# Where tiles begin in SBUF: a different start of weights and of moving operands within 512 bytes

## The chip, the core and the metric

The kernel runs on one core of a Trainium2 chip. The metric is the device time of one execution in microseconds (us), lower is better. Engines are named as in the profile: PE (TensorE matmuls), PEld (TensorE weight loads), DVE (VectorE), ACT (ScalarE), POOL (GpSimd), SP (the engine that issues most DMAs).

## What is computed

A decoder trunk of four layers on one sequence of 256 tokens, 1024 wide, in float32. Each layer is

```python
x = x + 0.5 * swiglu(rmsnorm(x), w_gu, w_down)      # ffn1, hidden width 2816
x = x + mixer(rmsnorm(x))                           # gated DeltaNet, stick-breaking, sparse, gated DeltaNet
x = x + 0.5 * swiglu(rmsnorm(x), w_gu, w_down)      # ffn2
```

and a last rmsnorm follows. Nearly all the work is in the products with the weights: in each of the eight feed-forward blocks 1024 x 5632 and 2816 x 1024, in each mixer the input and output projections.

## The kernel before

**Operands.** Everything is kept transposed, features on the 128 partitions and tokens along them, so a product has weights as its stationary operand (loaded by PEld) and activations as its moving operand (read by PE). A float32 operand is split into two float32r parts, hi and lo, and one product becomes three matmuls, hi*hi, lo*hi and hi*lo, added in PSUM (`mm3`, line 49).

**Weights.** `chunk` (line 160) brings 128 x 2048 float32 by one DMA of SP into a tile `r` (3 buffers) and splits it into four pieces of 512 columns: ACT writes `h` (line 170), DVE writes `l` (line 171), ten buffers of each. A weight load reads 128 columns of `h` or `l`, 512 bytes in each partition, at a multiple of 512 bytes from the piece's start. The exceptions are few: loads of 96 columns from the sparse mixer's `dsa_uk` pieces, at 0, 384, 768 and 1152 bytes of a piece; loads of 16 columns (`bah`, `bal`, DeltaNet's gates) and 8 columns (`wih`, `wil`, the sparse mixer's index weights) from small tiles; and the values' products of two mixers, where activations are loaded and weights are the moving operand of 512 columns.

**Moving operands.** `x2` holds the normed input, for each of the 8 k tiles 256 columns hi and 256 columns lo side by side (lines 215 to 223). In the feed-forward blocks `tile_wide` (line 284) multiplies a weight tile's hi part by all 512 columns and its lo part by the hi 256, two matmuls per k tile into a bank of kind G. `tiles2` (line 274) does the mixers' projections with three matmuls of 256 columns. `rows` (line 295) does the second product of a feed-forward block, whose moving operands are `ah` and `al` (256 columns each, into the four banks of kind A), and the output projections, whose moving operands are `oh` and `ol` (into banks of kind G). `lath` and `latl` are the sparse mixer's latents. The smaller products of the mixers use plain float32 or 16-bit tiles.

**Order.** One program order is written out by hand: big products in a row, and between groups of them `pump` (line 130) runs the next stages of side work (gates, norms, attention heads) whose due time, on a clock that `Bank.mm` counts, has come. The engines follow that order and wait for one another by semaphores. The change does not touch it, nor the number of buffers of any tile.

**Places in SBUF.** Tiles are laid one pool behind the other in each partition, in the order in which the pools are made (lines 72 to 77), and within a pool one group of buffers behind the other. The constants begin at byte 16,512 and take 16,096 bytes. So the pool of `r` begins at 32,608, which is 352 modulo 512. Behind it come 3 x 8192 bytes of `r`, 10 x 2048 of `h`, 10 x 2048 of `l`, 16,384 of `x2`, 8 x 8192 of the tiles called `b8` (`oh`, `ol`, `lath`, `latl`, queries, keys and others), and 6 x 2048 of the 512-column working tiles `w5`: all are multiples of 512, so every one of these tiles begins at 352 modulo 512. Then small tiles of 2240 bytes come in between, and `ah` (6 x 1024) and `al` (6 x 1024) lie at 32 modulo 512. `wih` and `bah` begin at 0 modulo 512.

In what follows the distance of a matmul is the start of its moving operand less the start of the weights that are loaded while it runs (those of the matmul after it), modulo 512. It is 0 for all big products on `x2`, `oh`, `ol`, `lath`, `latl`, and 192 for those on `ah` and `al`.

```python
    def mm3(self, out, w, x, stop):
        self.mm(out, w[0], x[0], False)
        self.mm(out, w[1], x[0], False)
        self.mm(out, w[0], x[1], stop)
```

Of the kernel before, what the change touches and what calls it, by code (L numbers as in the profile page):

```python
# [20 lines left out]
P = 128  # L21
T = 256          # tokens
D = 1024
KT = D // P      # k tiles of the model width
F = 2816
NS = F // 256    # steps of a feed-forward block, 256 hidden columns each
# [3 lines left out]
RS = 1024.0      # scale of the residuals kept in float16  # L30

# Everything is kept transposed: [feature on partitions, token].  A float32 matmul operand x is split
# exactly into hi = x rounded to float32r and lo = x - hi; hi*hi + lo*hi + hi*lo in PSUM carries float32.


class Bank:
    """One PSUM bank that several accumulation groups share."""
# [16 lines left out]
    def tr(self, out, x):  # L54
        """Transposes a [128, 128] float32 tile; the only kind of write to its part of the bank."""
        self.nc.tensor.transpose(out, x, self.k.ident)  # L56
        self.k.now += 0.11
# [8 lines left out]
class Trunk:  # L66

    def __init__(self, tc, ctx, a):
        self.tc, self.nc, self.a = tc, tc.nc, a
        nc = self.nc  # L70
        pool = lambda **k: ctx.enter_context(tc.tile_pool(**k))
        self.const = pool(name="const", bufs=1)
        self.raw = pool(name="raw", bufs=3)
        self.hip = pool(name="hi", bufs=10)
        self.lop = pool(name="lo", bufs=10)
        self.big = pool(name="big", bufs=8)
        self.wk = pool(name="wk", bufs=2)
        self.ps = pool(name="ps", bufs=4, space=bass.MemoryType.PSUM)
        self.side, self.now = [], 0.0
        self.act_set("silu_and_others")  # L80
        c = self.const
        self.x = c.tile([P, KT, T], F32, name="x")
        self.gains = c.tile([P, 13, KT], F32, name="gains")
        self.ones = c.tile([P, P], F32, name="ones")
        nc.gpsimd.memset(self.ones, 1.0)
        self.ident = c.tile([P, P], F32, name="ident")
        bf = c.tile([P, 2, P], BF16, name="bf")
        self.identb, self.scap = (bf[:, i] for i in range(2))
        hf = c.tile([P, 3, P], F16, name="hf")
        self.identh, self.identk, self.m1 = (hf[:, i] for i in range(3))  # L90
        self.consts = ((self.ident, a["ident"]), (bf, a["bf"]), (hf, a["hf"]))
        self.pad = c.tile([P, T], F32, name="pad")
        nc.gpsimd.memset(self.pad, 0.0)
        self.pcs = [c.tile([P, 2, 3 + T], F32, name="pc%d" % i) for i in range(2)]
        for pc in self.pcs:
            nc.gpsimd.memset(pc[:, :, :3], 0.0)

    def table(self, name):
        """A mixer's constants, side by side."""
        t = self.wk.tile([P, 1024], F32, name="tab", tag="tab", bufs=1)  # L100
        src = self.a[name]
        self.nc.sync.dma_start(t[:, :src.shape[1]], src)
        return t
# [4 lines left out]
    def w5(self, name, dt=F32):  # L108
        return self.wk.tile([P, 512], dt, name=name, tag="w5", bufs=6)

    def w2(self, name, dt=F32, tag="wa"):
        return self.wk.tile([P, 256], dt, name=name, tag=tag, bufs=6)
# [4 lines left out]
    def bank(self, tag="A"):  # L117
        """A: small products and a feed-forward's sums; G: the big projections."""
        return Bank(self, self.ps.tile([P, 512], F32, name="bank" + tag, tag=tag))

    # ---- interleaving: side work (generators) advances between groups of the big products.  A generator
    # yields how long (us on TensorE's clock, as counted here) its next stage's operands are expected to take,
    # or a condition that its next stage waits for.
# [6 lines left out]
    def pump(self, n=None):  # L130
        """Run up to n ready stages; only the first few (width) generators are under way."""
        for _ in range(n or self.burst):
            g = min(self.side[:self.width], key=self.due, default=None)
            if g is None or self.due(g) > self.now:
                return
            self.step(g)
# [8 lines left out]
    def wait(self, done):  # L145
        """Run side work until done()."""
# [13 lines left out]
    def chunk(self, src, w=2048, pw=512, pool=(), parts=1):  # L160
        """A [128, w] chunk of weights as (hi, lo) pieces of pw columns; the pieces in pool are split by GpSimd."""
# [12 lines left out]
    def first_chunk(self, src, n):  # L174
        """The kernel's start: the first chunk and x arrive in parts and are split as they come."""
# [27 lines left out]
    def rsqrt(self, a, n):  # L203
        """Newton's iteration for a ** -0.5 on a small tile."""
# [20 lines left out]
    def norm_in(self, n):  # L225
        """x times the gain, split; the tokens' factors come later (rstd)."""
# [5 lines left out]
    def spread(self, cols):  # L232
        """[token, 1] columns (SBUF) -> a bank with each as a row on all partitions."""
# [5 lines left out]
    def rstd(self, st):  # L239
        """1 / rms(x) per token, into st: compact [token, 2] and as rows [128, T]."""  # L240
# [28 lines left out]
    # GDN's chunks of the input projection, (kind, head pair): keys 0, values 1, queries 2, gate 3  # L269
    gdn_order = ((0, 0), (0, 1), (0, 2), (3, 0), (0, 3), (3, 1), (2, 0), (1, 0), (1, 1), (1, 2), (1, 3),  # L270
                 (2, 1), (3, 2), (2, 2), (2, 3), (3, 3))
    korder = (0, 2, 4, 6, 1, 3, 5, 7)    # the order in which a block's last products finish x

    def tiles2(self, pieces, xg, order=None):
        """Two M tiles (8 k tiles each) of one chunk into one bank."""
# [8 lines left out]
    def tile_wide(self, pieces, m, order=None):  # L284
        """One M tile into a bank: the columns of hi * hi and those of hi * lo + lo * hi side by side."""
# [9 lines left out]
    def rows(self, acc, pieces, a2, last, done=None):  # L295
        """acc[d, t] += w[f, d] a[f, t] for the chunk's two k tiles."""
# [73 lines left out]
    def gdn(self, i, n):  # L370
# [17 lines left out]
        # b and a: [16, T]  # L388
# [4 lines left out]
        # pairs (head, chunk of tokens) are kept in the order of the projections: head pair, chunk, head of the pair  # L393
# [13 lines left out]
        def gates():  # L407
# [29 lines left out]
            # E[j, i] = exp(G_i - G_j) for i >= j, else 0; eGb: exp(G_i) of the second chunk as rows  # L437
# [13 lines left out]
        def conv2(b, kind, c, dst):  # L451
            """Convolution and silu of two projected heads: dst [128, 2, T]."""
# [3 lines left out]
            # chunks are stored k, v, q; the convolution's channels q, k, v  # L456
# [18 lines left out]
        def keys(c):  # L475
# [23 lines left out]
            # A = I + L (unit lower triangular), transposed, in two float16 parts  # L499
# [8 lines left out]
            # the inverse X of A in float16 by merging blocks; XT its transpose  # L508
# [26 lines left out]
            # float32: with R = I - A X, the inverse is X + X R + X R R (+ X R^3, below float32)  # L535
# [7 lines left out]
            X1 = self.wk.tile([P, 4, P], F16, name="X1", tag="wb", bufs=6)  # L543
# [38 lines left out]
        def delta(c):  # L582
# [36 lines left out]
            # the queries' factor s = dk^-0.5 / |q| goes into the output's norm: s * rsqrt(s^2 ss/128 + eps)  # L619
# [53 lines left out]
    def sb(self, n):  # L673
# [31 lines left out]
        def attend(h, qk):  # L705
            # z^T: [keys, queries]; columns: key tile 0 x all queries, key tile 1 x queries of tile 1
# [38 lines left out]
    def rms_factor(self, sq, n, ones, out):  # L745
        """rsqrt(mean of squares + eps) per token from a squared tile, into out [token, 2]."""
# [11 lines left out]
    def dsa(self, n):  # L758
# [15 lines left out]
        # tiles of the input projection: cq 0..2, index key | rotary key 3, ckv 4..5; 6: the normed index key  # L774
# [25 lines left out]
        def weights():  # L800
            """A query's weights of the index heads, times the factor of its latent, which relu lets through."""
# [6 lines left out]
        def latents(c, b):  # L808
            """Evacuate a chunk of the input projection: factor of the token, squares, gain and split."""
# [21 lines left out]
        def index_keys():  # L831
            """kidx[:, e]: the rotated index key in the rows of a tile's head e, zeros in the other's; rotary keys into K."""
# [49 lines left out]
        def select():  # L882
            """The 64 largest of each row are struck out; what is struck out and causal is selected: neg 0, else -1e30."""
# [33 lines left out]
        def attend(h):  # L917
# [21 lines left out]
            for i in range(3):       # (key 0, query 0), (key 0, query 1), (key 1, query 1)  # L939
# [26 lines left out]
        # the index first, so that the selection runs beside the projections of queries, keys and values  # L966
# [61 lines left out]
    def final(self, out):  # L1028
        """The last norm, beside the last products: to be called with each tile of x as it is done."""
# [53 lines left out]
def cols(w):  # L1083
    """[1024, n * 256] -> [n, 128, 2048]: per chunk two M tiles of 8 k tiles."""
# [4 lines left out]
def rows(w):  # L1089
    """[n * 256, 1024] -> [n, 128, 2048]: per chunk two k tiles."""  # L1090
# [4 lines left out]
def pack_ffn(gu, down):  # L1095
    out = np.empty((gu.shape[0], NS, 3, 128, 2048), gu.dtype)
    for l in range(gu.shape[0]):
        # a chunk: gate tile, up tile
# [6 lines left out]
def feat(g):  # L1105
    """[n * 128] -> [128, n]"""
    return g.reshape(-1, 128).T


def pack(x, ffn1_norm, ffn1_w_gu, ffn1_w_down, mix_norm, ffn2_norm, ffn2_w_gu, ffn2_w_down,  # L1110
# [41 lines left out]
    # constants of the shapes  # L1152
# [10 lines left out]
    for v, s in enumerate((2, 4, 8, 16, 32, 64)):  # L1163
        c = np.arange(64)
        blk = c // s                      # block of 2s of the c-th first-half column
# [41 lines left out]
```

## Time and profile before

| what | value |
|---|---|
| time, median of 3 runs | 2089.65 us (2089.23 to 2093.7) |
| the profiled execution, span from first to last instruction | 2092.3 us |
| PE busy | 2037.1 us, 97% |
| DVE busy | 1646.0 us, 79% |
| ACT busy | 1308.2 us, 63% |
| mean busy share of the 16 DMA engines, by the main queue's packets | 48.4% |
| mean granted TensorE clock | 0.993 |

The profiled execution has no time of its own beside its span; the span lies inside the spread of the timed runs. Matmuls are pipelined: a matmul's row shows a duration of some 280 ns for 256 columns, but the next one starts 113 to 120 ns later. How fast the products go is therefore read from the starts in the timeline or from a run of matmuls in the chain of work, not from the mean duration of one.

### The profile page before, as it was taken

The numbers are of one execution on the slowest core, as the hardware profiler recorded it, in microseconds if no ns is written. First come the engines' busy times: TensorE is split into PE (matmuls) and PEld (weight loads), VectorE is DVE, ScalarE is ACT, GpSimd is POOL, SyncE is SP. The second block draws the span as 40 slices with busy tenths as digits, with TensorE's granted clock in tenths as the row PEclk, the third lists the DMA queues.
The fourth block names the chain that finished last, engine by engine and source line by source line (L and its number), as shares of the span: only waits on it lengthen the run. The fifth ranks groups of instructions, "written<-read, shape, count | busy, mean of one in ns | idle before, by whom it ended". The sixth has DMA issues, their size and how long they took to land.

```text
span 2092.3 us, 38898 instructions
## 1 busy us (share of the span) xinstructions
PE 2037.1 (97%) x14762; PEld 1886.2 (90%) x14762; DVE 1646.0 (79%) x3456; ACT 1308.2 (63%) x2804; POOL 161.9 (8%) x145
## 2 busy tenths in 40 slices
PE   8999899999999999999999998999999998999998
PEld 7999899999999989999989997899989998999997
DVE  7778898877887776777787789877787788988776
ACT  6566776665665566655665664765665667766654
POOL 1001311100100010100010013100010013111000
PEclk9999999999999999999999999999999999999999
DMA  7555333555455554555555542455555553235552
GB/s 256 195 188 182 102 105 123 173 190 187 171 206 188 195 179 140 176 184 197 185 184 199 182 153 76 162 187 196 184 182 199 184 179 106 100 119 182 182 199 84
DMA packets 52603, 353.62 MB, mean 169 GB/s; under 512 B 6976, under 2 KB 7872, under 8 KB 10688
## 3 DMA queue, kind: packets, MB, share of 16 engines
q1 hardware_dynamic: 52128, 350.49, 48.4%
q8 instruction: 116, 1.90, 0.4%
q14 instruction: 71, 0.58, 0.1%
q10 hardware_dynamic: 288, 0.66, 0.1%
HBM read 350.07 MB, written 1.05 MB: 168 GB/s over the span
## 4 chain that ended last, share of the span: by engine, by line
PE 82%; DVE 12%; ACT 4%; issue 1%; POOL 0%; DMA 0%; SPq 0%; ACTq 0%; DVEq 0%; POOLq 0%
PE bankG L43 55%; PE bankA L43 25%; DVE l L171 5%; ACT x L222 1%; DVE kT L466 1%; PE bankA L56 1%; ACT h L170 1%; DVE x L223 1%; DVE rs_t L211 1%; DVE x L302 0%; DVE rs_y L212 0%; DVE rs_t L210 0%; ACT sq L244 0%; DVE vT L466 0%; DVE pc L455 0%
## 5 line engine op out<-in xcount | busy, mean ns | idle before, releaser
L43 PE MATMUL bankG<-x,h 128*128 128x512 f32 (+1 forms) x4192 | 1269.0, 361 | 12.0 <-DVE x L223 12.0
L171 DVE TENSOR_TENSOR l<-r,h 128x512 fp32r<-128x512 f32 x1328 | 936.7, 713 | 374.1 <-ACT h L170 370.9
L170 ACT ACTIVATE h<-r 128x512 fp32r<-128x512 f32 x1328 | 823.0, 627 | 595.5 <-PE bankG L43 337.4
L43 PE MATMUL bankG<-x,l 128*128 128x256 f32 x3504 | 989.2, 282 | 0.0
L43 PEld LDWEIGHTS bankG<-x,h 128*128 128x128 f32 x4192 | 751.3, 189 | 130.1 <-DVE x L223 14.9
L43 PEld LDWEIGHTS bankG<-x,l 128*128 128x128 f32 x3504 | 666.5, 190 | 0.1
L43 PE MATMUL bankA<-ah,l 128*128 128x256 f32 x1408 | 389.2, 276 | 0.0
L43 PE MATMUL bankA<-ah,h 128*128 128x256 f32 x1408 | 389.2, 276 | 0.0
L43 PE MATMUL bankA<-al,h 128*128 128x256 f32 x1408 | 389.1, 276 | 0.0
L43 PEld LDWEIGHTS bankA<-ah,h 128*128 128x128 f32 x1408 | 264.4, 188 | 3.3
L43 PEld LDWEIGHTS bankA<-al,h 128*128 128x128 f32 x1408 | 264.5, 188 | 0.0
L43 PEld LDWEIGHTS bankA<-ah,l 128*128 128x128 f32 x1408 | 264.4, 188 | 0.0
L330 DVE TENSOR_TENSOR e<-e,bankG 128x256 f32<-128x256 f32 x352 | 145.9, 414 | 4.6 <-ACT e L329 4.6
L329 ACT ACTIVATE e<-bankG 128x256 f32<-128x256 f32 x352 | 129.3, 367 | 11.5 <-PE bankG L43 11.5
L245 POOL TENSOR_TENSOR sq<-sq 128x512 f32<-128x512 f32 x12 | 15.5, 1294 | 1473.8 <-ACT sq L244 1473.8
L342 DVE TENSOR_TENSOR e<-e,rb 128x512 f32<-128x512 f32 x176 | 121.0, 691 | 5.3 <-ACT rb L259 0.2
L199 ACT ACTIVATE ah<-e 128x256 fp32r<-128x256 f32 x176 | 72.6, 417 | 21.4 <-DVE e L344 21.3
L343 ACT ACTIVATE e<-e 128x256 f32<-128x256 f32 x176 | 71.3, 405 | 7.2 <-DVE e L342 7.2
L43 PE MATMUL bankG<-oh,h 128*128 128x256 f32 x256 | 74.5, 291 | 0.0
L344 DVE TENSOR_TENSOR e<-e 128x256 f32<-128x256 f32 x176 | 73.8, 419 | 0.7 <-ACT e L343 0.7
L200 DVE TENSOR_TENSOR al<-e,ah 128x256 fp32r<-128x256 f32 x176 | 73.1, 419 | 0.5 <-ACT ah L199 0.5
L43 PE MATMUL bankG<-oh,l 128*128 128x256 f32 x256 | 72.5, 283 | 0.0
(290 smaller groups left out, 1704.7 us busy)
## 6 DMA issues: line engine op xcount, KB each, us to landing
r<-in_ffn SPq DMA_DIRECT2D x262, 1024.0 KB, 4.9
r<-in_gdn_in SPq DMA_DIRECT2D x32, 1024.0 KB, 4.9
r<-in_gdn_out SPq DMA_DIRECT2D x8, 1024.0 KB, 4.9
r<-in_sb_qk SPq DMA_DIRECT2D x8, 1024.0 KB, 4.9
r<-in_sb_v SPq DMA_DIRECT2D x4, 1024.0 KB, 4.9
r<-in_sb_out SPq DMA_DIRECT2D x4, 1024.0 KB, 4.9
r<-in_dsa_out SPq DMA_DIRECT2D x4, 1024.0 KB, 4.9
r<-in_dsa_in SPq DMA_DIRECT2D x3, 1024.0 KB, 4.8
```

Source lines behind the costliest of these rows:

```text
L43: self.nc.tensor.matmul(out, lhsT, rhs, start=self.fresh, stop=stop, skip_group_check=True)
L56: self.nc.tensor.transpose(out, x, self.k.ident)
L170: self.nc.scalar.activation(h[:, :pw], src, AF.Copy)
L171: (self.nc.gpsimd if pool else self.nc.vector).tensor_sub(l[:, :pw], src, h[:, :pw].bitcast(F32))
L199: self.nc.scalar.activation(dh, src, AF.Copy)
L200: self.nc.vector.tensor_sub(dl, src, dh.bitcast(F32))
L211: nc.vector.scalar_tensor_tensor(t, t, -0.5, a, op0=ALU.mult, op1=ALU.mult)
L329: nc.scalar.activation(e[:, m * T:(m + 1) * T], b.t[:, :T], AF.Copy)
L330: nc.vector.tensor_add(e[:, m * T:(m + 1) * T], e[:, m * T:(m + 1) * T], b.t[:, T:])
L342: nc.vector.tensor_mul(e2, e2, st["rb"][:, None, :].to_broadcast([P, 2, T]))
L343: nc.scalar.activation(e[:, :T], e[:, :T], AF.Silu)
L344: nc.vector.tensor_mul(e[:, T:], e[:, T:], e[:, :T])
```

## The change

Two tiles that nothing uses are put in, one of 160 bytes per partition ahead of the pool of `r` and one of 256 bytes behind the pool of `l`, and the 512-column and 256-column working tiles get pools of their own behind the `b8` tiles, with the same six buffers for each tag. `X1`, which shared its buffers with `al`, goes along.

```diff
@@ Trunk.__init__
         self.const = pool(name="const", bufs=1)
+
+        pool(name="gap", bufs=1).tile([P, 40], F32, name="gap")
         self.raw = pool(name="raw", bufs=3)
         self.hip = pool(name="hi", bufs=10)
         self.lop = pool(name="lo", bufs=10)
+        pool(name="gap1", bufs=1).tile([P, 64], F32, name="gap1")
         self.big = pool(name="big", bufs=8)
+        self.w5p = pool(name="w5p", bufs=6)
+        self.w2p = pool(name="w2p", bufs=6)
         self.wk = pool(name="wk", bufs=2)
...
     def w5(self, name, dt=F32):
-        return self.wk.tile([P, 512], dt, name=name, tag="w5", bufs=6)
+        return self.w5p.tile([P, 512], dt, name=name, tag="w5")
 
     def w2(self, name, dt=F32, tag="wa"):
-        return self.wk.tile([P, 256], dt, name=name, tag=tag, bufs=6)
+        return self.w2p.tile([P, 256], dt, name=name, tag=tag)
...
-            X1 = self.wk.tile([P, 4, P], F16, name="X1", tag="wb", bufs=6)
+            X1 = self.w2p.tile([P, 4, P], F16, name="X1", tag="wb")
```

Comments are taken out too, which compiles to nothing. No instruction, no size and no order changes. With 160 more bytes `r` begins at 32,768, a multiple of 512, and so do `h` and `l`; with 256 more `x2`, `oh`, `ol`, `lath`, `latl` and `w5` begin at 256 modulo 512, and `ah` and `al`, which now follow `w5` directly, too. The distance of all big products becomes 256. All other tiles of the last pool move by 416 bytes modulo 512, as `x2` and the `b8` tiles do, so their places relative to those stay.

## Rows read from the trace of the kernel before

**Rows 1.** The page: span, and busy time, share and instructions of PE and DVE.
```profile
span 2092.3 us, 38898 instructions
...
PE 2037.1 (97%) x14762; PEld 1886.2 (90%) x14762; DVE 1646.0 (79%) x3456; ACT 1308.2 (63%) x2804; POOL 161.9 (8%) x145
```

**Rows 2.** The page: the chain that ended last, by engine and by line.
```profile
PE 82%; DVE 12%; ACT 4%; issue 1%; POOL 0%; DMA 0%; SPq 0%; ACTq 0%; DVEq 0%; POOLq 0%
```

**Rows 3.** Chain in order of time, a feed-forward block: start us, us, matmuls in one piece.
```profile
52.53 5.45 PE bankA L43 x48
57.97 11.10 PE bankG L43 x64
```

**Rows 4.** PE's timeline in a DeltaNet projection (start us, us, instruction): distance 0.
```profile
247.82 0.28 PE L43 MATMUL bankG<-x,l 128*128 128x256 f32 x1
...
248.90 0.28 PE L43 MATMUL bankG<-x,l 128*128 128x256 f32 x1
```

**Rows 5.** PE's timeline, index weights: loads of 8 columns, moving operand in x2.
```profile
1244.73 0.28 PE L43 MATMUL bankA<-x,wil 128*8 128x256 f32 x1
...
1245.75 0.28 PE L43 MATMUL bankA<-x,wil 128*8 128x256 f32 x1
...
1246.10 0.28 PE L43 MATMUL bankA<-x,wil 128*8 128x256 f32 x1
```

**Rows 6.** PE's timeline in the values' products of the stick-breaking mixer: 512 columns, distance 0.
```profile
752.21 0.39 PE L43 MATMUL bankG<-l,x 128*128 128x512 f32 x1
...
753.57 0.39 PE L43 MATMUL bankG<-l,x 128*128 128x512 f32 x1
```

**Rows 7.** Groups by line, shapes apart: count, busy us, mean ns | idle before.
```profile
L43 PE MATMUL bankG<-x,h 128*128 128x512 f32 x2816 | 990.2, 394 | 11.7 <-DVE x L223 11.7
L43 PE MATMUL bankG<-x,l 128*128 128x256 f32 x3504 | 989.2, 282 | 0.0
...
L43 PE MATMUL bankA<-ah,h 128*128 128x256 f32 x1408 | 389.2, 276 | 0.0
...
L43 PE MATMUL bankG<-x,h 128*128 128x256 f32 x1376 | 278.9, 292 | 0.2 <-DVE x L223 0.2
...
L43 PE MATMUL bankG<-oh,h 128*128 128x256 f32 x256 | 74.5, 291 | 0.0
...
L43 PE MATMUL bankG<-lath,h 128*128 128x256 f32 x36 | 10.7, 297 | 0.0
```

**Rows 8.** PE's timeline, plain float32 products: distance 0 (kT), then 192 (u).
```profile
243.76 0.83 PE L43 MATMUL bankA<-kT 128*128 128x128 f32 x6
...
354.29 0.94 PE L43 MATMUL bankA<-u,E 128*128 128x128 f32 x7
```

**Rows 9.** Groups by line on DVE: all at 352 (L344), and with al, ah at 32 (L200).
```profile
L344 DVE TENSOR_TENSOR e<-e 128x256 f32<-128x256 f32 x176 | 73.8, 419 | 0.7 <-ACT e L343 0.7
L200 DVE TENSOR_TENSOR al<-e,ah 128x256 fp32r<-128x256 f32 x176 | 73.1, 419 | 0.5 <-ACT ah L199 0.5
```

**Rows 10.** Busy us in a feed-forward stretch: PE, PEld, DVE, ACT, POOL, clock, DMA share.
```profile
390.00:570.00 180.00, 179.35 (x1215) 164.44 (x1214) 138.84 (x265) 110.96 (x227) 2.89 (x3) 1.00 0.56 192
```

**Rows 11.** PE's timeline, dsa_uk: loads of 96 columns at distances 0, 128, 256, 384.
```profile
1287.02 0.28 PE L43 MATMUL bankG<-lath,l 128*96 128x256 f32 x1
...
1288.08 0.27 PE L43 MATMUL bankG<-lath,l 128*96 128x256 f32 x1
1288.19 0.28 PE L43 MATMUL bankG<-latl,h 128*96 128x256 f32 x1
```

**Rows 12.** Busy us, clock and DMA share as in rows 10, of 3.2 us in dsa_uk.
```profile
1283.40:1286.60 3.20, 3.20 (x18) 3.20 (x17) 3.17 (x17) 1.11 (x2) 1.28 (x1) 0.50 0.03 5
```

**Rows 13.** PE's timeline inside the stretch of rows 12.
```profile
1283.61 0.41 PE L43 MATMUL bankG<-latl,h 128*96 128x256 f32 x1
...
1284.03 0.41 PE L43 MATMUL bankG<-lath,l 128*96 128x256 f32 x1
```

## Prediction

> **What bounds the kernel now.** I read the page first: PE is busy 97% of the span, DVE 79% [rows 1]. Busy time of pipelined matmuls proves little, so the chain that ended last comes next: 82% of it is PE [rows 2]. The reader is to see that almost every microsecond is paced by one matmul following another, so the question is what sets the step from start to start. The chain in order of time gives that step inside a feed-forward block [rows 3]. The second products (`ah`, `al`, distance 192) run 48 matmuls in 5.45 us, 113.5 ns each for 256 columns. The first products (`x2`, distance 0) run 64 in 11.10 us; 32 of them have 512 columns and 32 have 256, so one pair takes 346.9 ns. The timeline of a DeltaNet projection, also at distance 0, has nine steps of 256 columns in 1.08 us, 120 ns each [rows 4]. The same size of matmul thus costs 113.5 or 120 ns, and the clock doesn't explain it (granted 1.00 in a feed-forward stretch, 2.4 GHz [rows 10]).
>
> Two things differ between the two paces: the distance, and the PSUM banks (kind A, kind G). The index weights help to tell them apart: moving operand in `x2`, as in the products at 120 ns, but with loads of only 8 columns. Their nine steps from 1244.73 to 1245.75 take 1.02 us, 113 ns each [rows 5]. So the place of `x2` alone does not make a matmul slow. A long weight load from an unlucky place does, or bank G does, since these products go to bank A. I take the first reading: the load of the next weights and the moving read run side by side from one partition's memory, and starts that agree modulo 512 get in each other's way.
>
> **The change part by part.**
>
> *Products at distance 0 that go to 256, with 256 columns.* In [rows 7] the projections have 1376 with `x,h` and 3504 - 2816 = 688 with `x,l`; the output projections have three groups of 256; the latents' loads of 128 columns three groups of 36. That is 2064 + 768 + 108 = 2940. If 256 serves as well as 192 does, each step falls from 120 to 113.5 ns: 2940 x 6.5 ns = 19.1 us.
>
> *The 2816 pairs of 512 and 256 columns.* They take 346.9 ns now [rows 3]. What 512 columns cost without a collision, no row shows. One end: a fixed 113.5 - 106.7 = 6.8 ns above the columns' time for a matmul of any width (106.7 is 256 columns at 2.4 GHz; at 1.2 GHz the same products step by 0.42 us in two, 210 ns each, which is 256 columns and no excess, [rows 12, 13]). Then 512 columns cost 220.1, the pair 333.6, and the gain is 2816 x 13.3 ns = 37.5 us. Other end: the excess grows with the columns, 512 cost 227, the pair 340.5, and the gain is 2816 x 6.4 = 18.0 us. The nearest row is the values' product: 512 columns, six steps in 1.36 us, 226.7 each, and that at distance 0 [rows 6]. It fits the second end, with no collision left in a matmul long enough to cover its load. I take 18.0 us, and nothing for the values' products themselves.
>
> *The second products, from distance 192 to 256.* There are 3 x 1408 = 4224 [rows 7]. They are at the floor already; I take 0. The bounds are no gain below 113.5, and +6.5 ns each if 256 collides as 0 does (rival 2).
>
> *Working tiles, other engines, DMAs.* The plain float32 products don't care: six at distance 0 begin and end within 0.83 us, seven at 192 within 0.94; with 275 ns for the last, both give 111 ns a step [rows 8]. Zero for them. DVE takes 419 ns for 256 columns whether its tiles lie at 352 or at 32 [rows 9]; zero there too. DMAs, their number and order stay, and the DMA engines are busy 56% in a feed-forward stretch [rows 10]. Buffer counts stay, so no wait is added and none removed.
>
> *Does the gain reach the end?* In a feed-forward stretch of 180 us PE is busy 179.35, DVE 138.84, ACT 110.96 [rows 10]. PE's work there would shrink by about 2%, to some 176 us; DVE keeps more than 35 us of slack, which is the cover that the whole gain stands on. What is late next would be DVE's splitting `l`, but only if PE lost over a fifth. In the mixers some waits on side work grow by what the products give back; I take off nothing, as it is a part of at most a few us.
>
> *Sum.* 19.1 + 18.0 = 37.1 us. The traced span of 2092.3 becomes 2055.2. The median of the runs is 2089.65, 2.65 us lower, so against it the forecast is 2052.5.
>
> **A rule against it.** The rows show two paces for one shape, 113.5 and 120 ns [rows 3, 4]. The Trainium skill, "SBUF — State Buffer", section "Who interferes with whom", says that PE has two independent read ports, one for the moving operand and one for weight loads, and that PE never waits on anyone. By that rule places in SBUF cost PE nothing and the sum would be 0; it is rival 3 below. The rows don't refute it, since bank and distance differ together.
>
> **Rivals.**
>
> 1. *The excess is fixed per matmul.* The pairs gain 37.5 us, the sum is 19.1 + 37.5 = 56.6, the time 2033. For it: uniform. Against: 226.7 ns for 512 columns would then hide a second collision [rows 6]. Beyond it lies one more case: starts at multiples of 256 bytes instead of 32 past a multiple of 64 might remove the 6.8 ns itself. In units of 256 columns there are 2 x 2816 + 3504 + 1376 + 4224 + 768 + 108 = 15,612 of them, 106 us at most. The index weights' loads begin at many places and never go below 113 [rows 5], but their moving operand doesn't move. I give it 4%.
>
> 2. *256 is as bad as 0 (slower).* What counts may be the distance modulo 128 or 256, and then 192 was a lucky place. The big products on `x2` keep their pace, and the 4224 second products fall from 113.5 to 120 ns: 27.5 us, from 2089.65 to 2117. It decides from the first feed-forward block on, and all of it is in the runs of 48. For it: the `dsa_uk` products load 96 columns at distances 0, 128, 256 and 384, and the nine steps from 1287.02 to 1288.08 average 118 ns, so the places other than 0 gain little [rows 11]. Also, among the index weights' loads at eight places, the three steps from 1245.75 to 1246.10 take 117 ns where the nine before took 113; there the load begins at 96, which is just the distance 256 [rows 5]. Against: the one step of 110 ns in `dsa_uk` (1288.08 to 1288.19) is also the third and last with a load at 256 under way, as if the products were settling into a good place; the change of distance every three matmuls lets none of the four settle. And 192, which is close to 256, is good in 4224 cases, where 128 and 384 stand on the side of 0. If nearness to 0 is what hurts, 256 is the best place.
>
> 3. *Nothing.* The bank kind, not the place, makes the difference, or the loss at distance 0 has another cause. Then 2090. For it: all fast rows go to banks A. Against: no row shows anything that would make one kind of bank slower than the other.
>
> **How the numbers follow.** The forecast has 0.45, rival 1 with its extreme 0.11 (0.07 and 0.04), rival 2 has 0.32, rival 3 has 0.12. What a measurement of this kernel can tell from no change is about 0.2%, 4 us. So faster is 0.45 + 0.11 = 0.56, same 0.12, slower 0.32. Two signs hold most of the chance, so the likeliest case's own range stands apart: 2030 to 2060, from the fixed excess to a gain that the mixers' waits eat by 7 us. The whole range has to take in rival 2 with some us on its far side: 2025 to 2121; it leaves out the extreme of rival 1 and little else.
>
> **What would show each step right or wrong.** In the changed kernel's chain of waits in order of time, the runs of 64 should take 10.9 us (340.5 ns a pair) and those of 48 still 5.45; 10.68 would be rival 1, 11.10 with 5.76 rival 2, 11.10 with 5.45 rival 3. In the timeline the DeltaNet projections should step by 113 ns, the values' products by 227 as before, and the loads of PEld should still begin with the matmul before. DVE's mean of one split should stay. The forecast is wrong if the runs of 48 grow: then 256 is no good place. It is also wrong if PE's steps fall but its idle time grows by as much, so that another engine or a DMA took over.

## The result: slower, and the profile after

The changed kernel takes 2128.92 us (median of 4 runs, 2128.18 to 2132.45) where the kernel before takes 2091.68 in the same session (2089.23 to 2094.45): ratio 1.018, interval [1.0167, 1.0195]. The forecast was 2052.5; the time also lies beyond the range's upper end of 2121.

The page after: span and engines, then the chain that ended last by engine.

```profile
span 2126.4 us, 38898 instructions
...
PE 2073.3 (98%) x14762; PEld 1910.8 (90%) x14762; DVE 1645.6 (77%) x3456; ACT 1308.6 (62%) x2804; POOL 162.0 (8%) x145
...
PE 82%; DVE 13%; ACT 3%; issue 1%; POOL 0%; DMA 0%; SPq 0%; DVEq 0%; ACTq 0%; POOLq 0%
```

Against [rows 1, 2] only PE has changed: 36 us more busy time, with the same instructions and the same share of the chain. The chain in order of time shows where (start us, us, matmuls in one piece; it answers to [rows 3]).

```profile
51.44 5.75 PE bankA L43 x48
57.19 11.31 PE bankG L43 x64
68.50 5.75 PE bankA L43 x48
```

A run of 48 second products went from 5.45 to 5.75 us, 120 ns each. A run of 64 first products went from 11.10 to 11.31, a pair from 346.9 to 353.4 ns. The second products fill 88 runs of 48, 88 x 0.30 = 26.4 us. Of the pairs only 2304 lie in whole runs of 64, 72 of them; the other 512 are at the beginnings of the blocks, with side work between them, and take no longer than before. Summed over the starts of all matmuls in the two traces, the second products lost 26.1 us and the pairs 13.3 us, 39.4 us together. A part came back through the clock: the granted clock was at its lower level, half, for 27.3 us of the execution before and for 18.8 us after (means of 0.9935 and 0.9956), so an estimate of 4 us (half of the difference) was lost less. That leaves some 35 us where the spans of these two executions differ by 34.1; the medians differ by 37.2.

PE's timeline in a DeltaNet projection (as [rows 4]), then the feed-forward stretch (as [rows 10]), then groups by line.

```profile
249.62 0.28 PE L43 MATMUL bankG<-x,l 128*128 128x256 f32 x1
...
251.78 0.28 PE L43 MATMUL bankG<-x,l 128*128 128x256 f32 x1
```

```profile
390.00:570.00 180.00, 179.90 (x1184) 163.96 (x1183) 134.19 (x256) 105.69 (x217) 0.84 (x1) 1.00 0.56 193
```

```profile
L43 PE MATMUL bankA<-ah,l 128*128 128x256 f32 x1408 | 398.4, 283 | 0.0
...
L205 DVE TENSOR_TENSOR al<-e,ah 128x256 fp32r<-128x256 f32 x176 | 73.1, 420 | 0.5 <-ACT ah L204 0.5
```

Eighteen steps in 2.16 us: the projections still take 120 ns, as at distance 0. In the feed-forward stretch PE works without a gap and gets through 1184 matmuls where it did 1215; DVE and ACT do less beside them, and no engine holds PE up. The second products' mean rose from 276 to 283 ns [rows 7]; DVE's split of `al` is unchanged [rows 9].

### The profile page after: what moved, and what is told of

The parts are those of the page before. It is cut to its first block, busy times and chain, and to the rows that moved or that the text cites. A ratio compares the mean times of both kernels' runs of the same rounds, so it can differ in the third digit from the quotient of the medians.

```text
span 2126.4 us, 38898 instructions
## 1 busy us (share of the span) xinstructions
PE 2073.3 (98%) x14762; PEld 1910.8 (90%) x14762; DVE 1645.6 (77%) x3456; ACT 1308.6 (62%) x2804; POOL 162.0 (8%) x145
## 3 DMA queue, kind: packets, MB, share of 16 engines
q1 hardware_dynamic: 52128, 350.49, 47.5%
## 4 chain that ended last, share of the span: by engine, by line
PE 82%; DVE 13%; ACT 3%; issue 1%; POOL 0%; DMA 0%; SPq 0%; DVEq 0%; ACTq 0%; POOLq 0%
PE bankG L43 54%; PE bankA L43 27%; DVE l L176 5%; DVE kT L471 1%; PE bankA L56 1%; DVE x L228 1%; ACT x L227 1%; DVE rs_t L216 1%; ACT h L175 1%; DVE rs_y L217 1%; DVE rs_t L215 0%; DVE qT L471 0%; ACT sq L249 0%; DVE e L335 0%; DVE vT L471 0%
## 5 line engine op out<-in xcount | busy, mean ns | idle before, releaser
L43 PE MATMUL bankG<-x,h 128*128 128x512 f32 (+1 forms) x4192 | 1283.9, 365 | 10.3 <-DVE x L228 10.2
L43 PEld LDWEIGHTS bankG<-x,h 128*128 128x128 f32 x4192 | 754.2, 190 | 139.7 <-DVE x L228 13.3
L43 PE MATMUL bankA<-ah,l 128*128 128x256 f32 x1408 | 398.4, 283 | 0.0
L43 PE MATMUL bankA<-ah,h 128*128 128x256 f32 x1408 | 398.2, 283 | 0.0
L43 PE MATMUL bankA<-al,h 128*128 128x256 f32 x1408 | 398.2, 283 | 0.0
L43 PEld LDWEIGHTS bankA<-ah,h 128*128 128x128 f32 x1408 | 269.7, 192 | 4.1
L43 PEld LDWEIGHTS bankA<-al,h 128*128 128x128 f32 x1408 | 270.0, 192 | 0.0
L43 PEld LDWEIGHTS bankA<-ah,l 128*128 128x128 f32 x1408 | 269.8, 192 | 0.0
```

Of the source, the lines that this page charges most:

```text
L43: self.nc.tensor.matmul(out, lhsT, rhs, start=self.fresh, stop=stop, skip_group_check=True)
```

## The experiments

Of the first four runs' theories, **A** says that the distance counts modulo 128, so that 0 and 256 are bad alike and 192 good; **B** that it counts modulo 512 as predicted, but that starts at multiples of 64 bytes hurt; **C** that the kind of PSUM bank decides.

### map: the pace by distance

Matmuls only, the rest of the computation left out: groups of 48 with three pieces of weights and two moving pieces by turns, one group per distance, the banks A to H in rotation.

```python
        for d in range(0, 512, 32):
            group(0, d, one, 48)       # 256 columns; weights at 0 modulo 512
        for d in range(0, 512, 32):
            group(32, d, one, 48)      # weights at 32
        for d in (16, 48, 80, 112):
            group(0, d, one, 48)
        for d in range(0, 512, 64):
            group(0, d, pair, 48)      # 512 and 256 columns by turns
        for d in range(0, 512, 64):
            group(32, d, pair, 48)
...
        for w0, d in ((0, 64), (32, 64)):
            group(w0, d, ((256, 8),), 48)    # loads of 8 columns
```

> Leaves out the whole computation: it loads x, fills two tiles from it, runs groups of 48 float32r matmuls back to back, each group at one distance (start of the moving operand less start of the weights, modulo 512) and with the weights at 0 or at 32 modulo 512, and writes x out. Theory A (the distance counts modulo 128): 256 columns step by 120 ns at distances 0, 128, 256, 384 and by 113.5 ns at 64, 192, 320, 448, whether the weights begin at 0 or at 32; the distances 32 and 96 stand between. Theory B (the distance counts modulo 512, and what hurt the changed kernel is that its starts are multiples of 64 bytes): with the weights at 32, only distances near 0 step by 120 and all from 128 to 384 by 113.5; with the weights at 0, moving operands at multiples of 64 step by 120 everywhere. Theory C (the kind of PSUM bank): the step follows the bank, which changes with each group over all eight, and not the distance.

The chain in order of time; the groups shown are, in order, 256 columns at distances 0, 192, 256 and 16, pairs at distance 0 with weights at 0 and then at 32, 24 matmuls of 512 columns at distances 0 and 192, and 256 columns with loads of 8 columns at distance 64, weights at 0 and at 32.

```profile
22.50 5.76 PE bankB L43 x48
...
56.72 5.65 PE bankH L43 x48
...
68.05 5.75 PE bankB L43 x48
...
204.62 5.44 PE bankB L43 x48
...
226.92 8.48 PE bankF L43 x48
...
294.62 8.33 PE bankF L43 x48
...
362.15 5.46 PE bankF L43 x24
...
378.72 5.60 PE bankA L43 x24
...
389.78 5.46 PE bankC L43 x48
...
400.79 5.76 PE bankE L43 x48
```

Distances 0 and 256 take the same 120 ns, and with the weights at 0 the steps of 288 to 480 repeat those of 32 to 224: for these products 256 is 0. The rotation has eight banks and the distances repeat after eight groups, so here each bank meets the same distance, modulo 256, every time; it is `history`, below, that has 120 ns at 0 and at 256 in banks A, C, E and G alike. C falls by bank B, which takes 120 ns at 0 and 256 and 113.3 at 16. B falls too: with the weights at 0 it has 120 everywhere, where 192 takes 117.8, and with the weights at 32 it has 113.5 at 256, which takes 119.9. But A falls as well: 128 takes 118.6, not 120, and 192, which takes 113.5 in the kernel before, takes 117.8 here. And distance alone gives no pace at all: pairs at distance 0 take 353 ns in one group and 347 in the other, 8-column loads at distance 64 take 113.8 and 120. Groups of 512 columns alone, one for each distance, are fastest where those of 256 are slowest: 226.9 ns at 0 and 256, 228.7 at 64, 232.5 at 128, 233.3 at 192.

### d192 and d192_at0: all products at distance 192

The changed kernel with the tiles of the moving operands at distance 192 instead of 256; in `d192` the weights stay at 352 (the tile `gap` is left out), in `d192_at0` at 0, so that all starts are multiples of 64.

```diff
-        pool(name="gap1", bufs=1).tile([P, 64], F32, name="gap1")
+        pool(name="gap1", bufs=1).tile([P, 48], F32, name="gap1")
```

> The kernel before with 192 bytes between the pool of l and that of x2, and the working tiles behind it as in the change: weights at 352, every moving operand at 32 modulo 512, distance 192 throughout. Theories A and B alike: the 2940 single products fall from 120 to 113.5 ns (19 us), the 2816 pairs from 347 to 340 or 334 ns (18 to 37 us), the second products stay at 113.5: 2092 becomes 2035 to 2055. Theory C: 2092, no change.

> The changed kernel with 192 bytes instead of 256 behind the pool of l: weights at 0, every moving operand at 192 modulo 512, distance 192 as in the run before it, but all starts are multiples of 64. Theory A: the same as with the weights at 352, 2035 to 2055. Theory B: all products stay at their pace of the changed kernel, about 2129.

2115.73 us, ratio 1.0118 [1.0101, 1.0135], and 2113.08, ratio 1.0109 [1.0093, 1.0124]. The chain of `d192`:

```profile
50.95 5.65 PE bankA L43 x48
56.60 11.31 PE bankG L43 x64
```

No theory had these times: for `d192` A and B have 2035 to 2055 and C has 2092, for `d192_at0` B has 2129. The mixers' 256-column products do go from 119.7 to 114.5 ns on the mean, but the feed-forward blocks lose in both kinds of runs. The second products are as far from their weights as in the kernel before, 192, even modulo 2048, and take 117.7 instead of 113.5. What changed for them is what runs before them: the pairs.

### undo_ah: the change without its move of ah and al

```diff
-        pool(name="gap1", bufs=1).tile([P, 64], F32, name="gap1")
+        pool(name="gap1", bufs=1).tile([P, 48], F32, name="gap1")
+        self.w2p = pool(name="w2p", bufs=6)
+        pool(name="gap2", bufs=1).tile([P, 16], F32, name="gap2")
         self.big = pool(name="big", bufs=8)
         self.w5p = pool(name="w5p", bufs=6)
-        self.w2p = pool(name="w2p", bufs=6)
```

> The changed kernel with the pool of ah and al alone moved, to 192 modulo 512 (distance 192), all else as changed (distance 256). Theory A: the runs of 48 second products go from 5.75 back to 5.45 us, 88 x 0.30 = 26 us: 2129 becomes 2102, and the pairs stay at 353 ns. Theory B: 192 is a multiple of 64 as 256 is, so no gain, 2129.

2090.89 us, ratio 1.0001 [0.9991, 1.001]. The chain:

```profile
51.72 5.45 PE bankA L43 x48
57.17 11.10 PE bankG L43 x64
```

The whole loss is gone, also that of the pairs, whose `x2` is still at distance 256; neither theory had that. The other small tiles of the last pool stay where the change put them, so the loss is not theirs. Moving `x2`, `oh`, `lath` and the weights was worth nothing either way. From here on theory **H** says that what ran before a matmul counts beside its own places, **P** that its own places alone set its pace.

### ah_only: that one move alone

The kernel before, with `ah` and `al` 64 bytes further on modulo 512 (the working tiles have their own pools, as in the change). Of the tiles of the big products no other moves; the small tiles of the last pool, now behind `ah` and `al`, move by 256 modulo 512. The steps of all products other than the feed-forward blocks' and the projections take 193 us of PE here and 195 in the kernel before, so these tiles bring no loss.

```diff
         self.w5p = pool(name="w5p", bufs=6)
+        pool(name="gap2", bufs=1).tile([P, 64], F32, name="gap2")
         self.w2p = pool(name="w2p", bufs=6)
```

> The kernel before, with one thing of the change alone: ah and al 64 bytes further on (96 modulo 512, distance 256); weights, x2, oh and lath stay at 352, distance 0. Theory H (what ran before a matmul counts as well as its own places, so that the second products set the pace of the pairs that follow them): the whole loss is here, runs of 48 in 5.75 us, runs of 64 in 11.31 although nothing of theirs has moved, about 2129 us. Theory P (the pace of a matmul is a matter of its own places alone): runs of 64 stay at 11.10, only the runs of 48 grow to 5.75, about 2117 us.

2131.12 us, ratio 1.019 [1.0175, 1.0205]. The chain:

```profile
50.83 5.75 PE bankA L43 x48
56.58 11.31 PE bankG L43 x64
```

H, to the digit: the pairs lose 0.21 us a run although none of their operands moved. P falls.

### history: the same group after different preludes

```python
        for kind, d in ((one, 0), (one, 192), (one, 256), (one, 64), (pair, 0), (pair, 192), (pair, 256)):
            for pk, pd in ((one, 0), (one, 16), (wide, 0), (wide, 192), (pair, 128)):
                group(0, pd, pk, 24)
                group(0, d, kind, 48)
```

> Matmuls without the rest of the computation, which is left out: seven kinds of groups of 48 matmuls (256 columns at distance 0, 192, 256, 64; pairs of 512 and 256 columns at 0, 192, 256), each five times at exactly the same places, after five different preludes of 24 matmuls (256 columns at distance 0 or 16, 512 columns at 0 or 192, pairs at 128). Theory H: the same group at the same places takes different steps after different preludes, for the single products some at 113.3 ns and some at 117.8 or 120, for the pairs some at 346.7 and some at 353.3. Theory P: the five repeats of a group agree within 0.3 ns.

The chain: first the five groups of 256 columns at distance 192, then four of the pairs at distance 0.

```profile
74.62 5.46 PE bankE L42 x48
...
82.88 5.66 PE bankG L42 x48
...
94.02 5.65 PE bankA L42 x48
...
105.28 5.45 PE bankC L42 x48
...
114.94 5.45 PE bankE L42 x48
```

```profile
222.01 8.48 PE bankC L42 x48
...
233.29 8.48 PE bankE L42 x48
...
247.24 8.47 PE bankG L42 x48
...
261.31 8.33 PE bankA L42 x48
```

The same 48 matmuls at the same addresses step by 113.3 or by 117.8 ns, according to what ran before them, and hold that pace to the end. Single products at 64 do the same. The 24 before them alone may not decide, as the prelude at 16 has itself two paces, some 117 and 119. The bank changes from group to group as well; `ffn_map`, below, repeats a group in the same banks. At 0 and 256 they take 120 after all five preludes: these places showed one pace, the worst. Pairs at 0 and 256 settle at 346.7 after one of the preludes (512 columns at 192) and at 353.3 after the others; pairs at 192 take 353.3 after all.

The kernel before had shown it. This is its own chain in order of time, the start of a later feed-forward block:

```profile
589.88 5.66 PE bankA L43 x48
595.53 11.29 PE bankG L43 x64
606.83 5.45 PE bankA L43 x48
612.28 11.10 PE bankG L43 x64
```

The block starts with the longer steps, settles into 5.45 and 11.10, and stays there; in five of the eight blocks the first run of 48 is so, in three the run of 64 behind it too. In the changed kernel nothing settles so: 72 whole runs of each kind, nine in each block, all step by 120.0 and 353.3.

### ffn_map: the two kinds of runs by turns

Only the matmuls of a feed-forward step (64 and 48, in the kernel's order), for 42 pairs of distances, each twice in a row.

```python
        for dx, da in pairs:
            for _ in range(2):
                first(dx)
                second(da)
```

> The matmuls of a feed-forward step alone (the rest of the computation is left out): 64 matmuls of the first products by turns of 512 and 256 columns, then 48 second products of 256 columns, twice, for seven distances of x2 and six of ah/al. Theory H: the pairs' step depends on the distance of ah/al too: 346.7 ns at (x2 0, ah 192) and (256, 192), 353.3 at (256, 256) and (0, 256); the second products 113.3 at (0, 192) and (256, 192), but 117.7 at (192, 192). Theory P: the pairs' step depends on the distance of x2 alone and the second products' on that of ah alone. Neither says whether a combination is under 346.7 and 113.3.

In this stretch of the chain the distance of `x2` is 0 throughout; that of `ah` is 192 up to 43.44 and 256 from 54.55 on.

```profile
38.00 5.45 PE bankA L37 x48
43.44 11.10 PE bankG L37 x64
54.55 5.75 PE bankA L37 x48
60.29 11.31 PE bankG L37 x64
```

The pairs take 11.10 after second products of 113.3 ns and 11.31 after second products of 120: the coupling of `ah_only`, in four lines. Steps in ns of the second repeat, once the first few of a run are past, worked out from the starts of the matmuls:

| x2, ah | pair | second product |
|---|---|---|
| 0, 192 and 256, 192 | 346.7 | 113.3 |
| 0, 256 and 256, 256 and 0, 0 | 353.3 | 120.0 |
| 192, 192 | 353.3 | 117.8 |
| 128, 192 | 350.9 | 117.8 |
| 0, 112 | 353.3 | 113.8 |
| 16, 192 | 346.7 | 113.3 |
| 16, 256 | 346.7 | 120.0 |

The micro-kernel gives the paces of the before, changed and `d192` kernels. No combination of the 42 settles below 346.7 and 113.3: for its feed-forward blocks the kernel before was at the best place tried. It isn't safe there: (0, 192), tried again right after (256, 256), took 353.3 and 117.8, then 353.3 and 113.3. These are the banks and the addresses of the table's (0, 192), so it is not the bank that selects. The chain there, from the last second products at 256 on:

```profile
1457.65 5.75 PE bankA L37 x48
1463.40 11.31 PE bankG L37 x64
1474.72 5.65 PE bankA L37 x48
...
1491.66 5.45 PE bankA L37 x48
```

And H isn't the rule that a pace always hands itself on: at (16, 256) the pairs stay at 346.7 beside second products of 120.

### mix, mix_again and mix112: what the forecast wanted, in the mixers alone

The feed-forward layout of before, with `b8` tiles (`oh`, `ol`, `lath`, `latl` among them) at distance 192 and `x2` begun 192 bytes (`off` = 48 columns; 0 in the feed-forward blocks) further on in the three kinds of mixers. `mix_again` is the same kernel; in `mix112` `off` is 28, 112 bytes.

```diff
-        self.x2 = self.big.tile([P, KT, 2 * T], F32R, name="x2", tag="xg", bufs=1)
+        x2 = self.xp.tile([P, KT * 2 * T + 48], F32R, name="x2", tag="xg")
+        self.x2 = x2[:, self.off:self.off + KT * 2 * T].rearrange("p (j t) -> p j t", j=KT)
...
     def gdn(self, i, n):
+        self.off = 48
```

> The kernel before with its feed-forward layout kept (x2 distance 0, ah and al 192), but oh, ol, lath, latl moved to distance 192, and x2 begun 192 bytes further on in the mixers only. If the paces of the runs above hold there (single products at 192 in the mixers 113.5 ns, the feed-forward blocks 5.45 and 11.10 us): 2832 products x 6.5 ns = 18.4 us less, about 2072. Rival under theory H: a mixer that ends in another pace carries it into the next feed-forward block, runs of 64 take 11.31 and of 48 5.65, and the time is 2090 to 2100.

2085.04 us, ratio 0.9972 [0.996, 0.9985]: faster than both kernels, though by a third of what was expected. Chain of a feed-forward block, then PE's timeline in a DeltaNet projection:

```profile
50.45 5.45 PE bankA L43 x48
55.90 11.10 PE bankG L43 x64
```

```profile
246.00 0.28 PE L43 MATMUL bankG<-x,l 128*128 128x256 f32 x1
...
248.82 0.28 PE L43 MATMUL bankG<-x,l 128*128 128x256 f32 x1
```

The feed-forward blocks keep their pace; the rival, in which a mixer spoils them, didn't come. Twenty-four steps in 2.82 us, 117.5 ns in this stretch: the products at 192 have two paces in the kernel as well. Over the steps of the mixers' 256-column products that follow one another at full clock the mean went from 119.65 to 114.64 ns, 2538 x 5.0 = 12.7 us, not 18.4. Another 212 steps are longer than 150 ns and gain nothing: most are the first step after a piece of side work, some 200 ns in both kernels, and some 20 lie at half clock, 213 ns each. Of the 12.7 the time shows 6.6. PE's waits outside the feed-forward blocks (its steps over 400 ns, less 150 ns each) are 49.3 us here and 45.5 in the kernel before. That faster products wait longer for side work fits the other traces too (42.3 to 46.5 us in the changed kernel, `undo_ah` and `ah_only`, whose mixers run at 120 ns, 47.5 to 48.9 in the `d192` runs, `mix_again` and `mix112`), but it leaves some 2 us of the 12.7 without an account.

> The kernel mix once more, in more rounds beside the next one: ratio 0.997 to the kernel before, single products of the mixers at full clock 114.6 ns on the mean (120 in the kernel before).

> As mix, but x2 begins 112 bytes further on in the mixers instead of 192 (oh, ol, lath, latl stay at distance 192). In ffn_map the second products at 112 took 113.3 to 113.8 ns after every pace of the pairs, those at 192 took 113.3 or 117.8. Theory H with 112 as a place with one pace only: the mixers' products on x2 stay at 113.3 to 113.8 through every interruption, mean 113.6 at full clock, 2064 x 1 ns = 2 us less than mix, about 2083. Rival: distance 112 has a second pace too once side work interrupts, mean 114.6 or more, the same time as mix.

2083.75 us, ratio 0.9972 [0.996, 0.9984], and 2084.40, ratio 0.997 [0.9959, 0.9982]. At 112 the mixers' products take 114.93 ns on the mean beside 114.78: no gain. With side work between them the products don't stay in one pace at either place.

## Why the prediction was wrong

**What bounds the kernel: right.** PE's step from start to start paces the end; the chain has PE at 82% before and after, and of the 39.4 us of longer steps the medians show 37.2.

**Bank or place: the right side, the wrong rule.** Places make the difference, not the kind of bank (`map`). But the prediction took the distance for the whole cause. In these runs places only allow certain paces: one at 0 and 256 for single products (120 ns), two at 192 and 64 (113.3 and 117.8), two for pairs at 0 and 256 (346.7 and 353.3); what ran before selects among them (`history`, `ffn_map`). Nor do the short loads of [rows 5] tell place from bank: in `map` 8-column loads took 113.8 ns in one group and 120 in another.

**The step that failed: "if 256 serves as well as 192 does".** It doesn't; in `map` 256 is no other place than 0. The argument against this, that 192 lies close to 256 and that nearness to 0 is what hurts, fell with the 120 ns at 96 and at 256. One step of 110 ns in [rows 11] was no evidence of a good place. The terms came out so:

- 2940 products at 256 columns: 19.1 us forecast, none measured (119.65 ns at full clock before, 119.6 after).
- 4224 second products: 0 forecast, 26.1 us lost. Rival 2 had priced this at 27.5.
- 2816 pairs: a gain of 18.0 us forecast, 13.3 us lost. No case had this term with this sign. The prediction gave every kind of product a pace of its own, and rival 2 left the pairs as they were because their distance would be as bad as before. But the pairs went at 346.9 only because of the pace of the second products between them [rows 3]. One run of 64 doesn't show that; it takes two paces of one kind of run, as at 589.88 and 606.83 in the chain of before, which the prediction didn't use. Two smaller faults are in the same term: it took all 2816 pairs at 346.9, where the 512 at the beginnings of the blocks took longer before the change too, and it saw a collision to remove, where `map` has 512 columns alone fastest at 0 and 256.

So rival 2 named the mechanism's first half and the side, and its 2117 fell short of the 2128.92 by 12 us, about what the pairs lost.

**The other terms at nothing: right.** DVE's splits stayed at 419 to 420 ns, and the chain's share of other engines barely moved.

**The rule weighed against it.** `ah_only` moves `ah` and `al` by 64 bytes modulo 512, and the time grows by 1.9% through PE's steps. The Trainium skill, "SBUF — State Buffer", section "Who interferes with whom", by which PE never waits on anyone, would have had no change; the measurement decides against it for these steps, though the runs don't show what it is that PE waits for.

**The range** ended at 2121 because its worst case had one term of loss where there were two.

## What to carry to other kernels

Where matmuls follow each other without a gap, look for the same kind of run at two different paces in one trace before giving it a price: if there are two, the pace is a state that neighbours can change, and a move is priced for the sequence, not for its own instructions. Try a layout with the kernel's sequence of matmuls and nothing else, at several distances, before moving tiles; here that gave the kernels' paces to within 0.2 ns. And move one group of tiles at a time: of the groups of tiles moved here one did all the harm.

## What was not expected of the hardware

The same 48 matmuls at the same addresses held 113.3 or 117.8 ns a step to their end, set by what ran before them (`history`). Distances 256 apart gave equal single steps at full clock (120.0 at 0 and 256, 118.6 at 128 and 384, weights at 0, in `map`). Where the granted clock was half, the mixers' products at distance 0 stepped by 213 ns (kernel before, some 20 steps), double the 106.7 that 256 columns take at 2.4 GHz, with no excess. What keeps a pace from one matmul to the next stays open; no run here shows it.
